# Sums of x2 in five tasks between the first groups' steps, later statistics, and another block order in the second feed-forward product

## The chip, the cores and the metric

The kernel runs on one core of one Trainium2 chip. The metric is device microseconds of one launch, from the kernel's first to its last instruction and what lies around them. The core has a matrix engine (TensorE, in the profile PE, with its weight loads as PEld), two engines for elementwise work (VectorE, DVE, and ScalarE, ACT), GpSimd (POOL), and SyncE, whose queue (SPq) issues every DMA of this kernel. Each engine executes its instructions in the order in which the program was laid out.

## The reference, cut to what matters

One transformer layer on x of 1024 tokens by 1024 features, float32: a mixer (an mLSTM and a latent attention), a cross-attention into 256 memory tokens, and a feed-forward part. The change touches the end of the cross-attention and the feed-forward part:

```
x = x + memory_cross_attention(rmsnorm(x, norm_x_g[l]), mem_n, ...)    # its last product is o @ wo_x
h = rmsnorm(x, norm_ffn_g[l])
x = x + jnp.square(jax.nn.relu(h @ w_ff1[l])) @ w_ff2[l]               # 1024 -> 4096 -> 1024
```

## The kernel before

Activations lie feature by token, split in two token halves of 512 (`h` = 0, 1) and eight feature blocks of 128 (`k`). x2, the input of the feed-forward part, is in the tiles `res` (`R[h][k]`). Every float32 product is made of three passes on rounded halves ("hi" and "lo"): `split` writes hi on ACT (a CAST) and lo on DVE (a subtraction), and three matmuls use hi·hi, hi·lo and lo·hi.

**Both feed-forward products are block products in seven multiplications instead of eight.** x2 is cut in four blocks B11, B21 (token half 0) and B12, B22 (token half 1); the scheme needs the sums T1 = B12 − B11, T2 = B22 − T1, T3 = B22 − B12, T4 = B21 − T2 of them, and sums S1 to S4 of the blocks of the weight.

- `wo_groups` (L1194): the last product of the cross-attention. Its eviction writes `res`, stores it to `x2d` in DRAM and adds up squares in `st`: ACT writes a square into the single buffer `sq`, DVE adds it to `st`. After the last block it gives two tasks to the weaver: `xs` (`stats_x2`, L1217: four small matmuls `vps`, a VectorE step into `v`, a power on GpSimd into `r`) and `xn` (`norm_x2`, L1221).
- `norm_x2`: four VectorE steps and a matmul (`xdg`, `bps`) spread 1/rms over the tokens, `res` is scaled, and the halves of the blocks are made: for h = 0 those of B11 and B21 (`xB`), for h = 1 T1, T2, T3, B22, T4 (`xT`, and `xB` for B22) in one task of 20 steps.
- The weaver (L59) is a planner with its own costs. It runs when the program is written out and decides in which order the steps of tasks are laid among the steps of the main product. `until` runs tasks until a named one is done. A scheduler behind it then fixes the order on each engine, and moves an instruction forward where it takes the engine to be idle.
- `lead` (L1472): the first three of eight groups of 512 hidden features (`q`) begin with the multiplications of B11 and B21, which need h = 0 alone: 12 steps of 12 matmuls (`gf<-xB,w1u`).
- `ffn` (L1483): waits for the whole task `xn1`, then takes the other steps: T1, T2, T3, B22, T4 of groups 0 to 2, and all seven of groups 3 to 7. `prep` (L1535) makes the halves `w1u` of a step's weights two steps ahead. `combos` (L1507) loads blocks of w_ff1 (`w1r`) and makes the sums of a group: S1 = A21 + A22 (the tile `S`), S3 = A11 − A21, S2 = A11 − S1, S4 = A12 − S2, the last three in place. Blocks A11 and A12 of group 0 are loaded a second time, into buffers (tag "W") that hold `res`. Squared hidden values go to DRAM as seven planes `hd`.
- The second product has seven multiplications of 16 units (`units`, i and c), 12 matmuls each (`gf<-hu,w2u`). `prep2` (L1624) makes the halves `hu` and `w2u` of a unit two units ahead; `combos2` (L1633) makes the sums of w_ff2 in place (`w2r<-w2r`); `evac2` (L1673) adds the four banks of a multiplication into the results Y, U, Z, W (`acc`) after its last unit. `PL` is the order of the multiplications; the first two add up in the same banks, each other one starts new banks, taken in turn from two pools of four.

Of the kernel before, what the change touches and what calls it, by code (L numbers as in the profile page):

```python
# [18 lines left out]
P = 128  # L19
NK = 8  # L20
# [161 lines left out]
class Trunk:  # L182
# [160 lines left out]
    def run(self):  # L343
# [70 lines left out]
        with ExitStack() as lctx:  # L414
# [14 lines left out]
            self.lead_load(0)  # L429
            wv.done["ffa"] = wv.now  # L430
# [763 lines left out]
    def wo_groups(self, h):  # L1194

        V, R = self.V, self.R
        loc = {}

        def evac(g):
# [21 lines left out]
    def norm_x2(self, h):  # L1221
# [3 lines left out]
        t = self.big("raw", "xdg")  # L1225
        self.diag4(t[:, 0], self.r2[h])
        self.spread(t[:, 1], t[:, 0])
        rb = t[:, 1]
        yield 0.85, {}

        def norm(k):
            V.scalar_tensor_tensor(R[h][k], R[h][k], self.vec("gffn", k), rb, ALU.mult, ALU.mult)

        def halves(n, src):
            u = self.big("x1" if h else "x0", "x" + n, F32R)
            self.split(u[:, 0], u[:, 1], src)
            X.setdefault(n, []).append(u)

        def sub(o, a, b):
            V.tensor_tensor(o, a, b, ALU.subtract)  # L1240
            return o

        B11, B21, B12, B22 = R[0][:4], R[0][4:], R[1][:4], R[1][4:]
        if h == 0:
            for k in range(NK):
                norm(k)
                halves("B11" if k < 4 else "B21", R[0][k])
                yield 0.0, {}
            return
        for k in range(4):  # L1250
            norm(k)
            halves("T1", sub(B11[k], B12[k], B11[k]))
            yield 0.0, {}
        for k in range(4):
            norm(4 + k)
            halves("T2", sub(B11[k], B22[k], B11[k]))
            yield 0.0, {}
        for k in range(4):
            halves("T3", sub(B12[k], B22[k], B12[k]))
            yield 0.0, {}  # L1260
        for k in range(4):
            halves("B22", B22[k])
            yield 0.0, {}
        for k in range(4):
            halves("T4", sub(B21[k], B21[k], B11[k]))
            yield 0.0, {}
# [171 lines left out]
    def lead_load(self, q):  # L1438
        if q == 0:
            self.X, self.lw, self.lu, self.C = {}, {}, {}, {}  # L1440
        if q < self.LEAD:
            self.lw[q] = [self.w1_tile(q, 11, "raw"), self.w1_tile(q, 12, "raw")]

    def lead_prep(self, n):
        q, i = n // 4, n % 4
        if q < self.LEAD:
            if i == 2:
                self.lead_load(q + 1)
            self.lu[n] = self.w1_halves(self.lw[q][i // 2], i % 2)
# [22 lines left out]
    def lead(self):  # L1472
        self.lead_prep(0)
        self.lead_prep(1)
        for n in range(4 * self.LEAD):
            self.lead_prep(n + 2)
            q, i, e = n // 4, n % 4 // 2, n % 2
            if n == 0:
                yield ["xn0"]
            self.early(q, i, e, self.lu.pop(n))  # L1480
            yield 2.72

    def ffn(self):  # L1483
        V, A, T, S = self.V, self.A, self.T, self.S
        self.wv.weave(self.lead(), 1.0)
        self.wv.until(["xn1"])
        X, C, W = self.X, self.C, {}

        def load(q, b):
            tag = "raw" if q == 0 and b in (21, 22) else "W"  # L1490
            W[q, b] = self.w1_tile(q, b, tag)
# [8 lines left out]
        steps = [(q, i, e) for q in range(self.NQ) for i in range(2 if q < self.LEAD else 0, 7) for e in range(2)]  # L1500
        first = {q: min(n for n, s in enumerate(steps) if s[0] == q) for q in range(self.NQ)}
        us, late = {}, {}
# [3 lines left out]

        def combos(q):  # L1507

            n = first[q] + (0 if q >= self.LEAD else -4)

            def s1():
                t = self.big("raw" if q == 0 else "W", "S1", F32, (P, 4, 256))
                V.tensor_tensor(t, W[q, 21], W[q, 22], ALU.add)
# [7 lines left out]
            w = lambda b: W[q, b]  # L1521
            at(n - 6, lambda: load(q, 11))
            at(n - 5, lambda: load(q, 12))
            at(n - 3, lambda: load(q, 21))
            at(n - 1, lambda: load(q, 22))
# [9 lines left out]
        def prep(n):  # L1535
            if n < len(steps):
                q, i, e = steps[n]
                a = ORDER[i][0]
                us[n] = self.w1_halves(W[q, int(a[1:]) if a[0] == "A" else a], e)
# [61 lines left out]
        PL = (("11", 0), ("12", 1), ("22", 3), ("S1", 4), ("S3", 6), ("S2", 5), ("S4", 2))  # L1601
        B, hr, u2 = {}, {}, {}

        def load_b(n):

            b, j = ("11", "12", "22", "21")[n // 8], n % 8
# [26 lines left out]
        def combos2(i, c):  # L1633

            if c % 2 == 0 or i < 2:
                return
            j = c // 2 - 1 if i == 2 else c // 2
            for j in ([j] if j >= 0 else []) + ([7] if i == 2 and c == 15 else []):
                if i == 2:
                    V.tensor_tensor(B["22", j], B["21", j], B["22", j], ALU.add)  # L1640
                    B["S1", j] = B["22", j]
                elif i == 3:
                    B["S3", j] = sub(B["21", j], B["11", j], B["21", j])
                elif i == 4:
                    B["S2", j] = sub(B["11", j], B["S1", j], B["11", j])
                elif i == 5:
                    B["S4", j] = sub(B["12", j], B["12", j], B["S2", j])
# [19 lines left out]
        def mms(i, c, o, w, h):  # L1667
            for n, (x, y) in enumerate(PASSES):
                go_on = i == 1
                T.matmul(banks[o], lhsT=w[:, x, o * P:(o + 1) * P], rhs=h[:, y, :],  # L1670
                         start=not go_on and c == 0 and n == 0, stop=c == 15 and n == 2, skip_group_check=go_on)

        def evac2(i, o):  # L1673
            U, Y, Z, R = (acc[a][o] for a in "UYZW")
            ps = banks[o]
            if i == 0:
                A.copy(U, ps)
            elif i == 1:
                add(R, ps, R)
                store(o, "W", 0, 0)  # L1680
                S.dma_start(R, self.x2d[1, 4 + o])
            elif i == 2:
                add(Y, ps, Y)
            elif i == 3:
                add(Z, ps, Z)
                add(R, ps, R)
            elif i == 4:
                add(R, ps, R)
                add(Y, ps, Y)
            elif i == 5:  # L1690
                add(U, ps, U)
                add(R, U, R)
                store(o, "W", 1, 1)
                add(Y, U, Y)
                store(o, "Y", 1, 0)
                add(Z, U, Z)
            else:
                for q in (slice(0, 256), slice(256, 512)) if o == 3 else (slice(0, HT),):
                    add(Z[:, q], ps[:, q], Z[:, q])
                    store(o, "Z", 0, 1, q)  # L1700
# [7 lines left out]
        for f in late.pop(0, []):  # L1708
            f()
        prep(0)  # L1710
        prep(1)
        for n, (q, i, e) in enumerate(steps):
# [87 lines left out]
```

## Time and profile before

| | us |
|---|---|
| median of 3 runs (lowest, highest) | 1281.69 (1280.64, 1283.23) |
| profiled execution | 1284.04 |
| its span, first to last instruction | 1282.0 |
| TensorE busy | 1238.5 |
| VectorE busy | 901.4 |
| ScalarE busy | 664.8 |

The profile lists per engine the busy time, and per instruction its start, its length, and how long the engine stood idle before it and what ended that. Instructions alike that follow each other are merged in a row ("x8"). PEclk is the TensorE clock that was granted: 1.00 is 2.4 GHz, 0.50 is 1.2 GHz.

### The profile page before, as it was taken

Reading aid. Unit: us, or ns where it says so; the run is one execution under the profiler, and the core shown is the slowest. Engines: PE = TensorE matmul, PEld = TensorE weight load, DVE = VectorE, ACT = ScalarE, POOL = GpSimd, SP = SyncE. Lnnn points to the kernel's source line nnn. Section 1 sums busy time; section 2 is a strip of 40 time slices with the busy share of each in tenths; the row PEclk is TensorE's granted clock in tenths of the full one; section 3 lists DMA queues with packets and bytes.
Section 4 is the critical chain, followed back from the end, with each engine's and each line's share of the span. In section 5 each row is a group of like instructions: output and inputs, shape, how many; then the busy total and the mean of one; then the engine's idle time right before and its main releaser. Section 6 shows DMA issues by size and latency. Waiting matters only on the chain.

```text
span 1282.0 us, 17593 instructions
## 1 busy us (share of the span) xinstructions
PE 1238.5 (97%) x6030; PEld 1015.8 (79%) x6030; DVE 901.4 (70%) x1931; ACT 664.8 (52%) x1540; POOL 72.3 (6%) x90
## 2 busy tenths in 40 slices
PE   7999999999999999999897999999999999999998
PEld 6777777777888878888775888888888888888877
DVE  5876797898766556668689776576656459974674
ACT  6466645688555445546454444544444443444432
POOL 1100100243100010000000000000000000000000
PEclk9999999999999999999898999999999999999999
DMA  7245433312134364333245554444399934333341
GB/s 244 82 126 187 142 90 108 132 51 83 51 107 125 106 194 128 108 123 124 74 132 180 181 194 151 167 145 143 120 324 314 331 100 163 99 99 99 99 148 65
DMA packets 113168, 180.65 MB, mean 141 GB/s; under 512 B 8472, under 2 KB 40120, under 8 KB 113080
## 3 DMA queue, kind: packets, MB, share of 16 engines
q1 hardware_dynamic: 113080, 179.55, 42.6%
q8 instruction: 47, 0.77, 0.3%
q14 instruction: 41, 0.34, 0.1%
HBM read 134.41 MB, written 45.11 MB: 140 GB/s over the span
## 4 chain that ended last, share of the span: by engine, by line
PE 78%; DVE 8%; DMA 4%; issue 4%; ACT 3%; POOL 1%; SPq 0%; POOLq 0%; DVEq 0%; ACTq 0%
PE gf L56 45%; PE g L56 20%; PE pAS L56 3%; PE po L56 2%; DMA xr<-in_xT_dram 1%; DVE res L56 1%; PE pPT L56 1%; DMA xt<-in_x_dram 1%; DVE wu L56 1%; PE pxo L56 1%; DVE acc L56 1%; PE pq L56 1%; PE pxS L56 1%; PE qkps L56 1%; ACT wu L56 1%
## 5 line engine op out<-in xcount | busy, mean ns | idle before, releaser
L56 PE MATMUL gf<-hu,w2u 128*128 128x512 f32 x1344 | 305.4, 389 | 3.6 <-DVE hu L56 3.2
L56 PEld LDWEIGHTS gf<-hu,w2u 128*128 128x128 f32 x1344 | 252.1, 188 | 56.8 <-DVE hu L56 3.6
L56 PE MATMUL gf<-xT,w1u 128*128 128x512 f32 x768 | 182.9, 398 | 8.4 <-ACT w1u L56 8.4
L56 PEld LDWEIGHTS gf<-xT,w1u 128*128 128x128 f32 x768 | 145.4, 190 | 43.7 <-ACT w1u L56 8.8
L56 ACT CAST hu<-hr 128x512 fp32r<-128x512 f32 x112 | 69.8, 624 | 171.9 <-PE gf L56 171.9
L56 PE MATMUL g<-wu,xs 128*128 128x512 f32 (+1 forms) x576 | 145.0, 404 | 9.1 <-ACT wu L56 6.1
L56 DVE TENSOR_TENSOR hu<-hr,hu 128x512 fp32r<-128x512 f32 x112 | 77.3, 690 | 100.6 <-ACT hu L56 100.6
L56 PEld LDWEIGHTS g<-wu,xs 128*128 128x128 f32 x576 | 108.7, 193 | 36.2 <-ACT wu L56 6.7
L56 PE MATMUL gf<-xB,w1u 128*128 128x512 f32 x576 | 135.2, 392 | 0.0
L56 PEld LDWEIGHTS gf<-xB,w1u 128*128 128x128 f32 x576 | 108.0, 188 | 24.4 <-issue 0.5
L56 ACT CAST w1u<-w1r 128x512 fp32r<-128x512 f32 x96 | 59.1, 619 | 118.1 <-PE gf L56 115.7
L56 PE MATMUL g<-yT,wu 128*128 128x512 f32 x384 | 107.5, 411 | 1.4 <-ACT yT L56 1.4
L56 DVE TENSOR_TENSOR wu<-raw,wu 128x512 fp32r<-128x512 f32 (+1 forms) x112 | 75.9, 679 | 46.7 <-ACT wu L56 46.3
L56 ACT CAST wu<-raw 128x512 fp32r<-128x512 f32 (+1 forms) x112 | 68.3, 613 | 67.0 <-PE g L56 50.1
L56 DVE TENSOR_TENSOR w1u<-w1r,w1u 128x512 fp32r<-128x512 f32 x96 | 66.1, 689 | 35.4 <-ACT w1u L56 35.1
L56 DVE TENSOR_TENSOR c<-gf,c 128x512 f32<-128x512 f32 x80 | 55.1, 688 | 44.7 <-PE gf L56 44.6
L56 PEld LDWEIGHTS g<-yT,wu 128*128 128x128 f32 x384 | 68.7, 192 | 13.4 <-ACT yT L56 1.9
L56 DVE TENSOR_TENSOR w2u<-w2r,w2u 128x512 fp32r<-128x512 f32 x112 | 76.7, 685 | 0.0
L56 ACT CAST w2u<-w2r 128x512 fp32r<-128x512 f32 x112 | 68.9, 615 | 4.4 <-PE gf L56 4.4
L56 ACT ACTIVATE c<-c 128x1024 f32<-128x1024 f32 x56 | 59.5, 1062 | 8.6 <-DVE c L56 6.2
L56 PE MATMUL g<-xs,wu 128*128 128x512 f32 x192 | 48.4, 402 | 0.4 <-ACT mraw L56 0.4
L56 PE MATMUL g<-oT,wu 128*128 128x512 f32 x192 | 47.2, 398 | 0.4 <-ACT oT L56 0.4
(430 smaller groups left out, 1876.2 us busy)
## 6 DMA issues: line engine op xcount, KB each, us to landing
hd<-c SPq DMA_DIRECT2D x56, 512.0 KB, 3.5
hr<-hd SPq DMA_DIRECT2D x56, 512.0 KB, 3.6
w1r<-in_w_dram SPq DMA_DIRECT2D x38, 512.0 KB, 3.8
w2r<-in_w_dram SPq DMA_DIRECT2D x32, 512.0 KB, 7.1
raw<-in_w_in_dram SPq DMA_DIRECT2D x48, 256.0 KB, 2.9
raw<-in_w_out_dram SPq DMA_DIRECT2D x32, 256.0 KB, 3.0
xr<-in_xT_dram SPq DMA_DIRECT2D x16, 256.0 KB, 3.4
xt<-in_x_dram SPq DMA_DIRECT2D x16, 256.0 KB, 3.4
```

What stands on the lines that cost most here:

```text
L56: return f(*args, **kw)
```

## The change

The change has three parts.

1. **Statistics.** `xs0` may not begin before the planner's time of "ffa" plus 3.5 us; the other work that is laid there comes first.
2. **Sums of x2.** `norm_x2` becomes `sums_x2`, two tasks for h = 0 (B1, B2) and five for h = 1 (T1, T2, T3, B22, T4), in a chain. The step loops of `lead` and `ffn` become one loop `body` that is woven with these tasks: in groups 0 to 2 a step asks only for the task of its own block (`NEED`). The steps stay in the same order. The scratch `xdg` moves from the tag "raw" to "L2". The sums S3, S2, S4 of group 0, and the second loads of its A11 and A12, come one to several steps later in the program.
3. **Second product.** The multiplications run in another order of planes and weight blocks; the sums of w_ff2 follow it. Multiplications 2, 4 and 5 (numbers of the new order: i = 1, 3, 4) add up in one set of banks, 3 and 6 in the other. The evictions have 33 additions on VectorE in place of 45 and 4 copies on ScalarE; the partial result that was stored and read back is gone, and the residuals are read one result at a time.

```diff
-            self.lead_load(0)
-            wv.done["ffa"] = wv.now
+            self.ffn_setup()
+            wv.done["ffa"] = wv.now + 3.5
...
-                    self.wv.add(f"xs{h}", self.stats_x2(h, loc["st"]), prio=self.prio["xs"], res=dict(m=1))
-                    self.wv.add(f"xn{h}", self.norm_x2(h), [f"xs{h}", "xb2" if h else "ffa"], prio=self.prio["xn"],
-                                res=dict(m=1))
+                    self.wv.add(f"xs{h}", self.stats_x2(h, loc["st"]), prio=self.prio["xs"], res=dict(m=1),
+                                need=[] if h else ["ffa"])
+                    for n, kk in (("B1", 0), ("B2", 4)) if h == 0 else (("T1", 0), ("T2", 4), ("T3", 0), ("B22", 4), ("T4", 0)):
+                        self.wv.add("x" + n, self.sums_x2(h, n, kk), self.x2need + [f"xs{h}", "xb2" if h else "ffa"],
+                                    prio=self.prio["xn"], res={} if self.x2need else dict(m=1))
+                        self.x2need = ["x" + n]
...
-        self.wv.weave(self.lead(), 1.0)
-        self.wv.until(["xn1"])
...
-            at(n + 1, put("S3", lambda: sub(w(21), w(11), w(21))))
-            at(n + 2, put("S2", lambda: sub(w(11), w("S1"), w(11))))
-            at(n + 3, put("S4", lambda: sub(w(12), w(12), w("S2"))))
+            at(n + 1 if q else n + 2, put("S3", lambda: sub(w(21), w(11), w(21))))
+            at(n + 2 if q else n + 3, put("S2", lambda: sub(w(11), W[q, "S1"], w(11))))
+            at(n + 3 if q else n + 4, put("S4", lambda: sub(w(12), w(12), W[q, "S2"])))
...
-        PL = (("11", 0), ("12", 1), ("22", 3), ("S1", 4), ("S3", 6), ("S2", 5), ("S4", 2))
+        PL = (("22", 3), ("11", 0), ("S1", 4), ("S2", 5), ("S3", 6), ("S4", 2), ("12", 1))
+        CONT = (3, 4, 5)
+        SET = (1, 0, 1, 0, 0, 1, 0)
...
             elif i == 5:
-                add(U, ps, U)
-                add(R, U, R)
-                store(o, "W", 1, 1)
-                add(Y, U, Y)
-                store(o, "Y", 1, 0)
-                add(Z, U, Z)
+                add(Z, ps, Z)
+                store(o, "Z", 0, 1)
...
+        NEED = (["xB1"], ["xB2"], ["xT1"], ["xT2"], ["xT3"], ["xB22"], ["xT4"])
+
+        def body():
+            for n, (q, i, e) in enumerate(steps):
...
+                if q < self.LEAD:
+                    yield NEED[i]
+                make(n, q, i, e)
+                yield 2.72
+
+        self.wv.weave(body(), 1.0)
...
-            if c == 0 and i != 1:
-                banks[:] = [self.bank(i % 2 == 0) for _ in range(4)]
+            if c == 0 and i not in CONT:
+                banks[SET[i]] = [self.bank(SET[i]) for _ in range(4)]
```

Three places show what moves. **TensorE at the statistics of token half 0** (`vps`), between the transposes `pxT`, the products `pxo` of the last two cross-attention blocks, and the products `g` of the last half of `wo_x`; rows with − are before, with + now:

```order
 L56 MATMUL pxT<-ident,xP 128x128 x8
-L56 MATMUL vps<-ones,st_6882 128x1 x4
 L56 MATMUL pxo<-xPT,vmem 128x128 x8
 L56 MATMUL pxT<-ident,xP 128x128 x8
 L56 MATMUL pxo<-xPT,vmem 128x128 x8
+L56 MATMUL vps<-ones,st_6882 128x1 x2
 L56 MATMUL g<-oT_6725,wu 128x512 x12
+L56 MATMUL g<-oT_6726,wu 128x512 x6
+L56 MATMUL vps<-ones,st_6882 128x1 x2
```

The `vps` stood ahead of two rounds of `pxo` and one of `pxT`, and now stands behind them, half of it inside the products `g`.

**VectorE at the sums of token half 1.** Before, `S` (the sum S1 of the weights of group 0, used by the first step on T1) stands behind all of these sums (`res<-res`):

```order
L56 TENSOR_TENSOR res<-res 128x512 x2
L56 TENSOR_TENSOR xB_7696<-res,xB_7696 128x512
L56 TENSOR_TENSOR xT_7700<-res,xT_7700 128x512
L56 TENSOR_TENSOR xT_7704<-res,xT_7704 128x512
L56 TENSOR_TENSOR xT_7708<-res,xT_7708 128x512
L56 TENSOR_TENSOR res<-res 128x512
L56 TENSOR_TENSOR S_7723<-w1r 128x1024
L56 TENSOR_TENSOR xT_7712<-res,xT_7712 128x512
L56 TENSOR_TENSOR w1r<-w1r 128x1024
L56 TENSOR_TENSOR w1u<-S_7723,w1u 128x512
L56 TENSOR_TENSOR w1r<-S_7723,w1r 128x1024
```

Now `S` stands among the halves of T2 (`xT_7718` and `xT_7723` are two of the four); the other sums of the weights (`w1r<-w1r` is S3, `w1r<-S` is S2, the next `w1r<-w1r` is S4) follow behind T3 and among B22:

```order
L56 TENSOR_TENSOR S_7614<-w1r 128x1024
L56 TENSOR_TENSOR xT_7718<-res,xT_7718 128x512
L56 TENSOR_TENSOR xT_7723<-res,xT_7723 128x512
L56 TENSOR_TENSOR w1u<-S_7614,w1u 128x512
```

```order
L56 TENSOR_TENSOR xT_7774<-res,xT_7774 128x512
L56 TENSOR_TENSOR xT_7778<-res,xT_7778 128x512
L56 TENSOR_TENSOR res<-res 128x512 x3
L56 TENSOR_TENSOR xT_7782<-res,xT_7782 128x512
L56 TENSOR_TENSOR xB_7799<-res,xB_7799 128x512
L56 TENSOR_TENSOR w1r<-w1r 128x1024
L56 TENSOR_TENSOR xB_7824<-res,xB_7824 128x512
L56 TENSOR_TENSOR w1r<-S_7614,w1r 128x1024
L56 TENSOR_TENSOR xB_7830<-res,xB_7830 128x512
L56 TENSOR_TENSOR w1r<-w1r 128x1024
L56 TENSOR_TENSOR w1u<-w1r,w1u 128x512 x4
```

Between these two fences stand 8 instructions. `S` moved ahead of the last sum of T2 and of all of T3, B22 and T4; S3, S2 and S4 stand among the halves of B22, ahead of the halves of T4 and of the last two sums T4.

**VectorE at the end of the sixth multiplication of the second product**, before:

```order
L56 TENSOR_TENSOR hu<-hr,hu 128x512
L56 TENSOR_TENSOR acc<-gf,acc 128x512 x2
L56 TENSOR_TENSOR acc<-acc 128x512 x6
L56 TENSOR_TENSOR acc<-gf,acc 128x512 x2
L56 TENSOR_TENSOR acc<-acc 128x512 x6
L56 TENSOR_TENSOR w2u<-w2r,w2u 128x512
```

and now, at the same place, with eight additions at the end of the fifth:

```order
L56 TENSOR_TENSOR hu<-hr,hu 128x512
L56 TENSOR_TENSOR acc<-gf,acc 128x512 x4
L56 TENSOR_TENSOR w2u<-w2r,w2u 128x512
L56 TENSOR_TENSOR hu<-hr,hu 128x512
L56 TENSOR_TENSOR w2u<-w2r,w2u 128x512
```

Sixteen additions between two halves became four. Elsewhere in the second product, 16 of the 32 sums of w_ff2 (`w2r<-w2r`) now stand between the halves of the first 22 units, from behind the tenth `w2u` on, where before only `hu` and `w2u` stand.

## Rows read from the trace of the kernel before

**Rows 1.** The page, busy time of the engines
```profile
PE 1238.5 (97%) x6030; PEld 1015.8 (79%) x6030; DVE 901.4 (70%) x1931; ACT 664.8 (52%) x1540; POOL 72.3 (6%) x90
```

**Rows 2.** Waits of TensorE after 600 us: total, times, longest
```profile
PE gf L56 <- ACT w1u L56: 8.4, 1, 8.4
PE vps L56 <- DVE st L56: 6.3, 1, 6.3
PE gf L56 <- DVE hu L56: 3.2, 1, 3.2
PE gf L56 <- DVE acc L56: 0.4, 1, 0.4
```

**Rows 3.** Windows: stretch, its length, busy time of engines, PEclk, DMA share, GB/s
```profile
617.00:619.00 2.00, 2.00 (x16) 1.89 (x14) 0.29 (x1) 0.54 (x2) 0.00 (x0) 0.80 0.00 0
...
622.00:645.00 23.00, 22.90 (x98) 18.24 (x98) 21.09 (x40) 13.49 (x26) 0.00 (x0) 1.00 0.17 58
...
692.20:693.20 1.00, 1.00 (x4) 0.76 (x4) 1.00 (x2) 0.96 (x2) 0.00 (x0) 0.65 0.43 146
...
1237.00:1241.00 4.00, 0.81 (x4) 0.34 (x4) 4.00 (x7) 0.71 (x2) 0.00 (x0) 1.00 0.70 262
```

**Rows 4.** Timeline at the first wait: start, length, engine, instruction, idle before
```profile
605.75 1.03 PE L56 MATMUL pxT<-ident,xP 128*128 128x128 f32 x8
...
607.17 1.08 ACT L56 COPY xPT<-pxT 128x512 f32<-128x512 f32 x2
...
612.31 0.69 DVE L56 TENSOR_TENSOR st<-st,sq 128x512 f32<-128x512 f32 x1 [0.69 <-ACT sq L56]
613.05 1.87 PE L56 MATMUL vps<-ones,st 128*128 128x1 f32 x8 [6.27 <-DVE st L56]
...
619.37 2.38 PE L56 MATMUL pxo<-xPT,vmem 128*128 128x128 f32 x16 [0.24 <-ACT xPT L56]
...
622.10 3.02 PE L56 MATMUL g<-oT,wu 128*128 128x512 f32 x12 [0.35 <-ACT oT L56]
```

**Rows 5.** Timeline around the second wait; last two: loads of w1r, KB and landing
```profile
652.85 1.02 PE L56 MATMUL vps<-ones,st 128*128 128x1 f32 x8
...
656.68 24.18 PE L56 MATMUL gf<-xB,w1u 128*128 128x512 f32 x104
...
672.18 0.69 DVE L56 TENSOR_TENSOR res<-res 128x512 f32<-128x512 f32 x1
...
687.29 1.22 DVE L56 TENSOR_TENSOR S<-w1r 128x1024 f32<-128x1024 f32 x1
...
688.54 1.14 ACT L56 CAST w1u<-S 128x512 fp32r<-128x512 f32 x2 [0.52 <-DVE S L56]
...
689.21 18.68 PE L56 MATMUL gf<-xT,w1u 128*128 128x512 f32 x72 [8.36 <-ACT w1u L56]
...
w1r<-in_w_dram SPq DMA_DIRECT2D x38, 512.0 KB, 3.8
...
DMA to landing us min/median/max: 6.7/7.5/7.7
```

**Rows 6.** Timeline of the second product; fourth row: landing of w2r, 955 to 1060 us
```profile
980.30 0.41 SPq L1610 DMA_DIRECT2D w2r<-in_w_dram  x1
...
986.31 0.69 DVE L56 TENSOR_TENSOR hu<-hr,hu 128x512 fp32r<-128x512 f32 x1 [1.42 <-ACT hu L56]
...
1052.92 2.49 DVE L56 TENSOR_TENSOR w2r<-w2r 128x1024 f32<-128x1024 f32 x2
...
DMA to landing us min/median/max: 5.0/6.9/7.9
...
1142.64 4.87 DVE L56 TENSOR_TENSOR acc<-gf,acc 128x512 f32<-128x512 f32 x8
...
1235.68 3.69 DVE L56 TENSOR_TENSOR acc<-acc 128x512 f32<-128x512 f32 x6
...
1240.63 37.51 PE L56 MATMUL gf<-hu,w2u 128*128 128x512 f32 x164 [3.19 <-DVE hu L56]
```

More of the change, by code (lines that the diff above doesn't have):

```diff
@@ L1219, in stats_x2, with sums_x2, sub @@
         yield 0.3, {}
-    def norm_x2(self, h):
+    def sums_x2(self, h, n, k0):
         V, R, X = self.V, self.R, self.X
[L1225 to L1234, printed above, removed]
+        if n in ("B1", "T1"):
+            t = self.big("L2", "xdg")
+            self.diag4(t[:, 0], self.r2[h])
+            self.spread(t[:, 1], t[:, 0])
+            self.rb2 = t[:, 1]
+            yield 0.85, {}
+        rb = self.rb2
+        def sub(o, a, b):
+            V.tensor_tensor(o, a, b, ALU.subtract)
+        B11, B21, B12, B22 = R[0][:4], R[0][4:], R[1][:4], R[1][4:]
+        for k in range(4):
+            if n in ("B1", "B2", "T1", "T2"):
+                r = R[h][k0 + k]
+                V.scalar_tensor_tensor(r, r, self.vec("gffn", k0 + k), rb, ALU.mult, ALU.mult)
+            if n == "T1":
+                sub(B11[k], B12[k], B11[k])
+            elif n == "T2":
+                sub(B11[k], B22[k], B11[k])
+            elif n == "T3":
+                sub(B12[k], B22[k], B12[k])
+            elif n == "T4":
+                sub(B21[k], B21[k], B11[k])
+            src = {"B1": B11, "B2": B21, "T1": B11, "T2": B11, "T3": B12, "B22": B22, "T4": B21}[n][k]
@@ L1235, in halves @@
             u = self.big("x1" if h else "x0", "x" + n, F32R)
             self.split(u[:, 0], u[:, 1], src)
[L1237 to L1265, printed above, removed]
+            X.setdefault({"B1": "B11", "B2": "B21"}.get(n, n), []).append(u)
@@ L1470, in plane @@
         self.S.dma_start(self.hd[i][2 * q:2 * q + 2].rearrange("n p c -> p n c"), t)
[L1472 to L1481, printed above, removed]
     def ffn(self):
         V, A, T, S = self.V, self.A, self.T, self.S
-        self.wv.weave(self.lead(), 1.0)
-        self.wv.until(["xn1"])
[L1487 to L1491, printed above, removed]
+        X, C, W, steps, us = self.X, self.C, self.W, self.steps, self.us
         def sub(o, a, b):
@@ L1633, in combos2 @@
         def combos2(i, c):
[L1635 removed]
+            if c % 2 == 0:
                 return
[L1637 to L1639 removed]
+            j = c // 2 - 1
+            for j in ([j] if j >= 0 else []) + ([7] if c == 15 else []):
+                if i == 1:
                     V.tensor_tensor(B["22", j], B["21", j], B["22", j], ALU.add)
                     B["S1", j] = B["22", j]
+                elif i == 2:
+                    B["S2", j] = sub(B["22", j], B["S1", j], B["11", j])
                 elif i == 3:
@@ L1707, in ffn @@
         at(N - 2, lambda: load_h(3))
[L1708 to L1712, printed above, removed]
-            for f in late.pop(n, []) if n else []:
-                f()
-            prep(n + 2)
-            if n >= N - 2:
-                prep2(n - N + 2)
-            make(n, q, i, e)
+        NEED = (["xB1"], ["xB2"], ["xT1"], ["xT2"], ["xT3"], ["xB22"], ["xT4"])
+        def body():
+            for n, (q, i, e) in enumerate(steps):
+                if n == 0:
+                    prep(0)
+                    prep(1)
+                for f in late.pop(n, []):
+                    f()
+                prep(n + 2)
+                if n >= N - 2:
+                    prep2(n - N + 2)
+                if q < self.LEAD:
[3 more added lines that the diff above has]
+        self.wv.weave(body(), 1.0)
         nb = 8
-        banks = [None] * 4
+        banks = [None, None]
         for n, (i, c) in enumerate(units):
```

88 lines of the change are left out of this document (46 added, 42 removed).

## The prediction, made before the changed kernel ran

> **What bounds the kernel now.** TensorE, by its own busy time: 1238.5 us of the span [rows 1]. So an edit gains only where TensorE stands still or runs at half clock. I read TensorE's waits first, for the part of the span that the change touches, from 600 us on: four, of 8.4, 6.3, 3.2 and 0.4 us, 18.3 in all [rows 2]. Then the windows around them, for the clock. After the 6.27 us wait the granted clock is 0.80 in 617 to 619, after the 8.36 us wait it is 0.65 in 692.2 to 693.2, and after the 3.19 us wait it is 1.00 [rows 3]. With two levels, 1.00 (2.4 GHz) and 0.50 (1.2 GHz), half clock ended 0.8 us into the first window and 0.7 into the second: it ran from 613.05 to 617.8 and from 689.2 to 692.9, 4.8 and 3.7 us, of which half is lost, 2.4 and 1.8. What can be won at most is 18.3 + 4.2 = 22.5 us. Last I read who is late in each wait, in the timelines [rows 4 to 6]; the number of matmuls stays as it is.
>
> **Statistics (term A).** The `vps` wait for `st`, whose last addition starts at 612.31: each of its four squares waits for the buffer of the one before, and VectorE idles 0.69 us each time [rows 4]. Meanwhile `pxo`, `pxT`, `pxo` and the products `g` stand behind `vps` on TensorE's queue, although the copies `xPT` end at 608.25. The change puts `vps` behind them. Walked by hand: `pxo` from 608.3; a round of 16 took 2.38 us at full clock with a wait of 0.24 in it [rows 4], so 2.2, to about 610.5; `pxT` 1.03, to 611.6; its copy and the next round, 612.3 to 614.6. The squares now alternate with the small `oT` steps on both engines, so `st` is done about 614.9; two `vps` and the first `oT` let `g` start at about 615.6 instead of 622.10: 6.5 us earlier. Of this, 1.2 us go back: half of `vps` (1.02 us whole at full clock [rows 5]) and a wait for `xdg` now lie inside `g`, and VectorE, which was busy 21.1 of 23.0 us in 622 to 645 [rows 3], has the same work for a shorter stretch. Its rows up to the second `vps`, 35 steps from 624.7 on at 0.62 (an estimate a little above the 0.60 that eight in a row take each [rows 6]) and 1.2 of waiting for evictions, give 647.6 for that `vps`, against 652.85 [rows 5]. So A = 5.3. Bounds: 2.9, if the clock falls all the same, and 6.5, if nothing is given back.
>
> **Sums (term B).** Everything from the second `vps` to the step on T1 keeps its distance, so I stay in the times of before. TensorE ends the steps on B11 and B21 at 680.85 [rows 5]. `S` stood behind all sums of x2 and ran at 687.29; now it stands right behind the sum that ran at 672.18, so it runs at 672.8, its halves are there by 677.7, and the 24 matmuls on T1 (0.233 each, from 24.18 us for 104 [rows 5], so 5.6 us) run from 680.85 to 686.4 without a wait. Then comes a new wait, the one thing the part does not remove: T2 needs S2 = A11 − S1, A11 needs a buffer that T3's first two halves set free, at 681.4 by the count of the rows, then a load, then the sums S3 and S2 (1.22 us each, a half between them) and the cast on ACT. The load: 3.8 us is the median of all 38, but 6.7 to 7.7 for the five that were issued together from 681.4 on [rows 5]. I take 4.5, nearer the first, because this load now goes out ahead of the others. A11 is there at 686.0, S2 at 689.0, the first half for T2 at 689.6. VectorE makes S4 before the lo halves of T2, so TensorE runs seven matmuls on hi halves and is in full flow from 691.3, which counts as a start at 689.7. T3 ends 48 matmuls later, at 700.9. Before, it ended at 707.9 (689.21 + 18.68 [rows 5]). So B = 7.0 by this walk; A12's load, which S4 needs and which is issued at 684.5 together with others, may be late by up to 2, so I take B = 6.5. Bounds: 3.0, with both loads at 7.5 us and some half clock, and 7.5. Behind T3, the steps on B22 and T4 find their halves ready by the same count (the last half of T4 at about 709, used at about 709), and the evictions into `c22`, which wait for buffers of `res` that T4 sets free, are 3 us ahead of their use.
>
> **Second product (term C).** The wait of 3.19 us comes from 16 additions in a row on VectorE (3.69 us for the last six [rows 6]) while `w2u` and `hu` of the next units stand behind. With 8 additions, 4.87 us, the row of before at 1142.64 has no wait on TensorE behind it [rows 2, 6]; the changed kernel has 8 at most. The 0.4 us came from a second set of banks out of the pool that had just been used, with two sums of weights in front of the evictions; the new sets alternate. So 3.6 us go. Against that, 16 sums of w_ff2 now lie in the first 22 units. Up to there VectorE has 16 × 1.2 + 25 × 0.60 + 4 × 0.60 = 36.6 us of work from about 987.5 on (pitches from [rows 6]); the half `hu` that unit 21 needs must be there by 1026.5, 39.0 later, and 2.4 us of cover are left for waiting on loads of `w2r`. The first such load is issued at about 980.3, as a load in that place is now, and lands 5.0 to 7.9 us later [rows 6]: 985 to 988, and the next, at about 984.8, by 993, used at about 991. I expect 1 to 3 us of waiting on VectorE and 0.6 on TensorE. C = 3.0; bounds 0 and 3.6. The four copies on ACT and the store and reload that go lie beside other work and are worth nothing.
>
> **The sum.** A + B + C = 5.3 + 6.5 + 3.0 = 14.8. Against the profiled execution, 1284.04 us: 1269.2. Its span is 1282.0, and 2.0 lie around it. The median of the runs is 1281.69, 2.35 below that execution, so I predict 1266.9 for the median.
>
> **Rivals.** *S2 is the new late one.* Both loads take 7.5 us and the clock falls in the gap, which is then over 5 us instead of 3: B = 3.0, the median 1270.4. For: the landings of 6.7 to 7.7 [rows 5]. Against: fewer loads are in flight.
>
> *The clock falls at the first place all the same.* TensorE there has transposes, small products and three gaps of 0.7 to 1.5 us in 9 us. A = 5.3 − 2.4 = 2.9 and the median 1269.3. Against it: 3.19 us of standing still left the clock at 1.00 [rows 3], but there full products ran on both sides. The Trainium skill ("TensorE: Matmul & The Clock Gate", Part 4) says that transposes do not count as activity for the clock; by that rule this case is the likelier, and the sum would be 12.4 instead of 14.8. No row before shows a stretch of this make-up, so its chance stays low.
>
> *The sums of w_ff2 hold up the second product.* VectorE takes its queue in order, so a sum whose load is late holds back `hu` and `w2u` of all later units. Once the 2.4 us of cover are used, each further microsecond reaches TensorE. With 4 us beyond it C = −0.4, and the median is 1270.3. **The slower outcome** is this one: it decides from 15.4 us of waiting beyond the cover (14.8 + 0.6), that is 2.2 us for each of the eight sums that need the third block, (15.4 + 2.4) / 8. Loads landing in 10 us instead of 7 would do it; at 3 us each, 24 − 2.4 − 15.4 = 6 us slower, 1288. Against: the slowest of 23 took 7.9 [rows 6].
>
> *It doesn't do what it says.* If the second loads of A11 and A12 hold SP's queue or the sums wait for each other, both waits are only moved: A and B vanish but for 1 us, C is 3.0 less 2, and the median is about 1280. Against: the order of instructions shows `S` and `vps` moved.
>
> **How the numbers follow.** The forecast, 1266.9, gets 0.62, with its own range of 1263.8 to 1269.5; S2 late 0.14, half clock at the first place 0.09, sums in the second product without a loss overall 0.06, no effect 0.05, slower 0.04. The range of 1263.5 to 1273.0 takes in the first four, and two of the middle cases together (1273). Below 1263.5 is only what needs all three upper bounds, 17.6. About 0.2%, 2.6 us, is what a measurement of this kernel can tell from no change. So: faster 0.91, same 0.05, slower 0.04.
>
> **What would show it.** Right: the wait of `vps` for `st` gone, PEclk 1.00 from 606 on; the first `gf<-xT` right behind the last `gf<-xB`, and one wait of about 3 us some 24 matmuls later, ended by `w1u`; no wait for `hu` at the end of the second product. Wrong, A: PEclk 0.50 around 612 to 618, or the second `vps` waiting for `st` over 1 us. Wrong, B: that wait over 5 us, or others at T4. Wrong, C: waits of `w2u` or `hu` between units 9 and 22, with VectorE waiting for `w2r` loads. The prediction as a whole fails if the middle of the first product, which had no wait from 741 to 969, gets any: then the moved loads cost what I took as free.

## The result, and the profile after

The changed kernel takes 1265.89 us (median of 4 runs, 1264.90 to 1267.75) against 1282.46 us for the kernel before (4 runs, 1280.64 to 1284.07). The ratio is 0.9863, 95% interval 0.9846 to 0.9879: 16.6 us faster. The forecast was 1266.9 us, range 1263.5 to 1273.0. Its profiled execution took 1264.90 us, with a span of 1263.1.

The page of the changed kernel, busy time; it answers to [rows 1]:

```profile
PE 1234.6 (98%) x6030; PEld 1011.2 (80%) x6030; DVE 894.9 (71%) x1919; ACT 662.0 (52%) x1536; POOL 72.6 (6%) x90
```

The number of matmuls is the same, and TensorE's busy time fell by 3.9 us only. Most of the rest of the gain is time in which it stood still. Its waits from 600 us on (total, times, longest), where [rows 2] had 8.4, 6.3, 3.2 and 0.4:

```profile
PE gf L56 <- ACT w1u L56: 2.1, 1, 2.1
PE pxo L56 <- ACT xPT L56: 1.3, 2, 1.0
PE bps L56 <- DVE xdg L56: 1.0, 2, 0.5
PE vps L56 <- DVE st L56: 0.4, 1, 0.4
```

The four old waits are gone; what is left is one of 2.1 us for `w1u` and small ones of 2.7 us in all. (The trace of before has three small ones too, which [rows 2] leaves out: `bps` 0.5, `g` 0.4, `pxo` 0.2.) TensorE's timeline of the changed kernel at the three places (start, length, instruction, idle time before it in brackets), which answers to [rows 4 to 6]:

```profile
603.70 1.03 PE L56 MATMUL pxT<-ident,xP 128*128 128x128 f32 x8
605.75 2.32 PE L56 MATMUL pxo<-xPT,vmem 128*128 128x128 f32 x16 [1.02 <-ACT xPT L56]
...
611.91 0.58 PE L56 MATMUL vps<-ones,st 128*128 128x1 f32 x4 [0.36 <-DVE st L56]
612.35 4.35 PE L56 MATMUL g<-oT,wu 128*128 128x512 f32 x18
...
644.39 1.05 PE L56 MATMUL vps<-ones,st 128*128 128x1 f32 x8
...
672.25 5.76 PE L56 MATMUL gf<-xT,w1u 128*128 128x512 f32 x24
680.10 13.17 PE L56 MATMUL gf<-xT,w1u 128*128 128x512 f32 x48 [2.09 <-ACT w1u L56]
...
954.46 304.82 PE L56 MATMUL gf<-hu,w2u 128*128 128x512 f32 x1344
```

`vps` now waits 0.36 us instead of 6.27. The products on T1 follow B11's and B21's at once, and T2 waits 2.09. The second product is one row of 1344 matmuls without a gap. The windows (PEclk is the number before the last two) tell where the clock stood:

```profile
609.00:613.00 4.00, 3.40 (x23) 2.96 (x24) 3.17 (x8) 2.50 (x9) 0.00 (x0) 1.00 0.97 329
613.00:619.00 6.00, 6.00 (x30) 5.00 (x29) 2.65 (x7) 3.49 (x8) 1.38 (x1) 1.00 0.22 77
...
680.00:683.00 3.00, 2.90 (x7) 1.80 (x7) 1.74 (x2) 1.61 (x4) 0.00 (x0) 0.58 0.88 305
680.50:683.90 3.40, 3.39 (x9) 2.17 (x8) 2.64 (x4) 1.11 (x3) 0.00 (x0) 0.50 0.64 220
683.00:685.00 2.00, 1.99 (x8) 1.56 (x8) 2.00 (x5) 0.00 (x0) 0.00 (x0) 0.77 0.11 28
685.00:690.00 5.00, 5.00 (x23) 4.08 (x22) 4.62 (x8) 1.25 (x2) 0.00 (x0) 1.00 0.64 202
```

At the first place it stays at 1.00, where [rows 3] had 0.80. Behind the wait at T2, which ends at 680.10, it falls to its lower level from 680.5 to 683.9. Only seven matmuls begin between 680 and 683, and that is the pace of this level: five of them in a row begin 0.43 us apart, where 0.23 us is the pace at 1.00. What T2 waited for is seen on SyncE's queue and VectorE (same columns as the timeline above; the first line is the issue of A11's load, the second begins with the issue of A12's):

```profile
672.88 0.37 SPq L1412 DMA_DIRECT2D w1r<-in_w_dram  x1
...
675.29 10.60 SPq L1412 DMA_DIRECT2D w1r<-in_w_dram  x5
...
664.36 1.21 DVE L56 TENSOR_TENSOR S<-w1r 128x1024 f32<-128x1024 f32 x1
...
676.43 1.23 DVE L56 TENSOR_TENSOR w1r<-w1r 128x1024 f32<-128x1024 f32 x1
...
678.18 1.22 DVE L56 TENSOR_TENSOR w1r<-S,w1r 128x1024 f32<-128x1024 f32 x1
...
681.26 1.23 DVE L56 TENSOR_TENSOR w1r<-w1r 128x1024 f32<-128x1024 f32 x1 [1.26 <-DMA w1r<-in_w_dram]
682.40 2.49 DVE L56 TENSOR_TENSOR w1u<-w1r,w1u 128x512 fp32r<-128x512 f32 x4
...
988.06 1.23 DVE L56 TENSOR_TENSOR w2r<-w2r 128x1024 f32<-128x1024 f32 x1 [1.03 <-DMA w2r<-in_w_dram]
```

The lines from 664.36 to 681.26 are S1, S3, S2 and S4 of group 0. S3 and S2 found A11 there, and the first half that T2 needs is made from S2, which ends at 679.40. S4 waited 1.26 us for A12's load, and the low halves that T2 needs stand behind it. On TensorE this late S4 shows in one place: the eighth matmul on T2 begins 0.63 us behind the seventh instead of 0.43, 0.2 us lost. The rest of its lateness lies under the half clock: at full clock the first seven would have been through about 1.4 us sooner (an estimate from the two paces), and TensorE would have stood still for the low halves. The last line is a sum of w_ff2 in the second product, which also waits for a load, with no wait on TensorE behind it.

Span against span the two executions differ by 18.9 us, and 2.05 of that are not the change's: the `pxT` ahead of the first wait begins at 605.75 before [rows 4] and at 603.70 after, with the same instructions in the same order up to there (TensorE, VectorE, ScalarE and GpSimd). So the experiments are compared by stretches between landmarks of TensorE's timeline: that `pxT` (the expectations call it the second transposes); the first matmul on B11; the first on T1; the first on B22; the first of the second product; its last.

### The profile page after: what moved, and what is told of

Its sections match the earlier page's. It is cut to its first block, busy times and chain, and to the rows that moved or that the text cites. A ratio compares the mean times of both kernels' runs of the same rounds, so it can differ in the third digit from the quotient of the medians.

```text
span 1263.1 us, 17573 instructions
## 1 busy us (share of the span) xinstructions
PE 1234.6 (98%) x6030; PEld 1011.2 (80%) x6030; DVE 894.9 (71%) x1919; ACT 662.0 (52%) x1536; POOL 72.6 (6%) x90
## 4 chain that ended last, share of the span: by engine, by line
PE 81%; DVE 7%; DMA 4%; issue 4%; ACT 3%; POOL 1%; SPq 0%; POOLq 0%; DVEq 0%; ACTq 0%
PE gf L56 46%; PE g L56 21%; PE pAS L56 3%; PE po L56 2%; DMA xr<-in_xT_dram 1%; PE pPT L56 1%; DVE res L56 1%; PE pxo L56 1%; DMA xt<-in_x_dram 1%; DVE wu L56 1%; PE pq L56 1%; ACT wu L56 1%; PE pyT L56 1%; PE pxS L56 1%; PE qkps L56 1%
```

## The experiments

Starts, differences of starts, and the end of the last matmul, in us, worked out from TensorE's timeline of each trace; the ratio is that of the times, against runs of before on the same chip:

| kernel | that pxT at | to B11 (A) | B11 to T1 | T1 to B22 | B11 to B22 (B) | B22 to second product | second product (C) | ratio to before, 95% |
|---|---|---|---|---|---|---|---|---|
| before | 605.75 | 39.33 | 44.13 | 18.52 | 62.65 | 261.39 | 309.02 | |
| before, again | 604.92 | 39.90 | 44.14 | 18.79 | 62.93 | 261.39 | 309.06 | 0.9993 (0.9977–1.0009) |
| C alone | 606.09 | 40.43 | 44.14 | 19.44 | 63.58 | 261.39 | 304.82 | 0.9953 (0.9936–0.9970) |
| A alone | 605.52 | 33.00 | 44.10 | 19.63 | 63.73 | 261.37 | 310.46 | 0.9954 (0.9938–0.9970) |
| A and C | 604.00 | 33.03 | 44.07 | 18.43 | 62.50 | 261.39 | 304.82 | 0.9896 (0.9877–0.9915) |
| B and C | 603.91 | 39.48 | 35.60 | 19.04 | 54.64 | 261.63 | 304.82 | 0.9879 (0.9862–0.9896) |
| changed (A, B, C) | 603.70 | 33.02 | 35.53 | 20.86 | 56.39 | 261.35 | 304.82 | 0.9863 (0.9846–0.9879) |
| changed, again | 607.00 | 33.03 | 35.56 | 20.85 | 56.41 | 261.36 | 304.82 | 0.9850 (0.9831–0.9869) |
| changed, third | 603.82 | 33.05 | 35.53 | 20.77 | 56.30 | 261.37 | 304.82 | 0.9851 (0.9828–0.9875) |
| early loads | 604.38 | 33.01 | 35.55 | 18.14 | 53.69 | 261.47 | 304.82 | 0.9827 (0.9809–0.9846) |
| early loads, again | 606.25 | 33.05 | 35.55 | 18.14 | 53.69 | 261.43 | 304.82 | 0.9834 (0.9812–0.9856) |
| and S1 on GpSimd | 604.36 | 33.05 | 35.54 | 23.69 | 59.23 | 264.27 | 304.82 | 0.9889 (0.9871–0.9906) |
| and other buffers for c12, c22 | 604.89 | 33.01 | 35.57 | 16.79 | 52.36 | 266.53 | 304.82 | 0.9858 (0.9841–0.9874) |

**C alone.** The hunks of the second product, on the kernel before:

```diff
-        PL = (("11", 0), ("12", 1), ("22", 3), ("S1", 4), ("S3", 6), ("S2", 5), ("S4", 2))
+        PL = (("22", 3), ("11", 0), ("S1", 4), ("S2", 5), ("S3", 6), ("S4", 2), ("12", 1))
+        CONT = (3, 4, 5)
+        SET = (1, 0, 1, 0, 0, 1, 0)
...
```

> The kernel before with the change in the second product alone (order 4 1 5 6 7 3 2, two sets of banks, the later loads and sums of w_ff2). Theory: three separate terms that add up, A (statistics) 6.4 us, B (sums in tasks) 6.2, C (second product) 4.2, as the two traces give them. Then this kernel keeps the waits of 6.3 us (vps for st) and 8.4 us (w1u) and loses the 3.2 and 0.4 us ones; the stretch of the second product is 304.8 us instead of 309.0; the time is 4.2 us below before (1282.5 to 1278.3, ratio 0.997). Rival: part of the 4.2 comes from what A and B left in front of the second product (buffers and loads that are earlier); then the stretch is 305.4 us or more, or waits for hu or w2u show in it.

The second product takes 304.82 us, to the hundredth what it takes in the changed kernel; the other two waits stand as before. TensorE's waits from 600 us on in this kernel:

```profile
PE gf L56 <- ACT w1u L56: 8.4, 1, 8.4
PE vps L56 <- DVE st L56: 6.3, 1, 6.3
```

C is worth 4.2 us against the first trace of before, and needs nothing of A or B.

**A alone.**

```diff
-            wv.done["ffa"] = wv.now
+            wv.done["ffa"] = wv.now + 3.5
...
-                    self.wv.add(f"xs{h}", self.stats_x2(h, loc["st"]), prio=self.prio["xs"], res=dict(m=1))
+                    self.wv.add(f"xs{h}", self.stats_x2(h, loc["st"]), prio=self.prio["xs"], res=dict(m=1),
+                                need=[] if h else ["ffa"])
```

> The kernel before with the statistics' two edits alone (the normalisation's due time 3.5 us later, and the squares of the first half held back to it). Theory of separate terms: the wait of vps for st goes, the clock stays at 1.00 from 606 to 619, the second vps comes 6 us earlier, the wait at T1 stays at about 8.4 us with its stretch of half clock: 6.4 us below before (1276.1, ratio 0.995). Rival, VectorE carries the stretch: the sums of x2 end no earlier than before because VectorE, not TensorE, sets them; then the wait at T1 grows by what was won at vps, and the gain is 0 to 2 us.

The stretch to B11 falls to 33.00 us, 6.3 below the first trace of before, and B11 to T1 stays at 44.10: the wait of 8.4 us moves along whole and does not grow, so VectorE does not carry that stretch. The trace brought one thing that was not asked for. Its wait for `hu` in the second product is the old one of 3.19 us, but here the clock fell behind it (window of this kernel):

```profile
1235.00:1238.00 3.00, 2.87 (x7) 2.29 (x8) 3.00 (x6) 0.00 (x0) 0.00 (x0) 0.50 0.12 36
```

and the second product took 310.46 us instead of 309.02.

**A and C, B left out.** The edits of the two kernels above together.

> The kernel before with the statistics and the second product changed, and the sums of x2 as they were (A and C without B). Separate terms: only the wait of 8.4 us for w1u at T1, with its stretch of half clock, is left of the four; the time is 10.6 us below before (6.4 + 4.2; ratio 0.992) and 6.2 above the changed kernel (1.005). Rival, B is worth more than its 6.2 because the clock fell at T2 in the changed kernel's trace and need not: up to 9 us above the changed kernel.

Of the four old waits the 8.4 us one alone is left. B11 to B22 takes 62.50 us, so that B, beside A and C, is worth 6.2 (62.50 − 56.3). In time this kernel is 0.9896, the changed one 0.9850 in the same comparison: 0.5%, 5.9 us, as the separate terms have it (6.2). Against before the times give 13.4 us where the terms have 10.6, and the stretches 10.6 (6.30 + 0.15 + 4.20).

**B and C, A taken out of the changed kernel.** The two edits of A put back.

> The changed kernel with the statistics put back where they were (sums in tasks and second product as changed, B and C). Separate terms: the wait of vps for st is back with about 6.3 us and the granted clock near 0.8 in the two microseconds behind it, and the time is 6.4 us above the changed kernel (1272.3, ratio 0.992 to before). Rival, the terms depend on each other: with x2 later by 6 us against the loads, A11's and A12's second loads have more time, the wait at T2 is smaller, and the time is only 3 to 5 us above the changed kernel.

The wait for `st` is back, and the stretch to B11 takes 39.48 us again. But B11 to B22 takes 54.64, 1.7 us less than beside A. TensorE's timeline of this kernel, and then the window behind T2's wait:

```profile
678.99 5.76 PE L56 MATMUL gf<-xT,w1u 128*128 128x512 f32 x24
686.57 11.63 PE L56 MATMUL gf<-xT,w1u 128*128 128x512 f32 x48 [1.82 <-ACT w1u L56]
```

```profile
687.00:692.00 5.00, 5.00 (x23) 3.76 (x22) 5.00 (x9) 1.70 (x4) 0.00 (x0) 1.00 0.97 315
```

T2 waits almost as long (1.82 against 2.09), yet 48 matmuls take 11.63 us instead of 13.17, and the clock stays at 1.00. S4 here waits for no load. This is the one trace of this kernel. So the rival holds in part: A is worth 6.3 without B, and 6.46 − 1.75 + 0.28 = 5.0 with it, the middle figure being B11 to B22 and the last the stretch behind it. B is worth 8.0 without A (62.65 − 54.64) and 6.2 with it; the kernels without B spread from 62.50 to 63.73 in this stretch, by the length of their half clock. In time this kernel lies 0.0016 to 0.0029 above the three ratios of the changed kernel, 2.1 to 3.7 us, with intervals that overlap; the figure of 5.0 rests on the stretches alone.

**Early loads of A11 and A12.** On the changed kernel; S3, S2 and S4 of group 0 at the steps of the other groups.

```diff
             if q == 0:
-                at(n, lambda: self.load_w1(q, 11))
-                at(n + 1, lambda: self.load_w1(q, 12))
+                at(2, lambda: self.load_w1(q, 11, "x1"))
+                at(3, lambda: self.load_w1(q, 12, "x1"))
...
-            at(n + 1 if q else n + 2, put("S3", lambda: sub(w(21), w(11), w(21))))
+            at(n + 1, put("S3", lambda: sub(w(21), w(11), w(21))))
...
```

> The changed kernel with one more edit: group 0's second loads of A11 and A12 go into two buffers of x2's sums (T4's last tiles take others later) and are issued some 6 steps earlier, and its sums S3, S2, S4 go one step earlier, as in the other groups. Theory: what is left at T2 (a wait of 2.09 us for w1u, seven matmuls on high halves with a wait for low ones, the clock at 0.58 and 0.77 up to 685) comes from the late buffer and load of A11 and A12. Then T2 follows T1 with no wait over 0.3 us, the clock stays at 1.00, and the matmuls on B22 begin up to 3.9 us earlier: 1262.0 us, ratio 0.984 to before. Rival, VectorE is the bound there (it was busy without a gap from 675 to 680): the sums of weights that now run earlier push back the sums of x2 behind them, the wait moves to T2's or T3's own halves, and the gain is 0 to 1 us.

TensorE's timeline of this kernel, and then a window:

```profile
672.94 16.96 PE L56 MATMUL gf<-xT,w1u 128*128 128x512 f32 x72
691.08 5.82 PE L56 MATMUL gf<-xB,w1u 128*128 128x512 f32 x24 [1.18 <-DVE c L56]
```

```profile
672.00:691.00 19.00, 17.90 (x77) 14.08 (x75) 18.93 (x33) 12.51 (x22) 0.00 (x0) 1.00 0.42 138
```

T1, T2 and T3 run as one row of 72 matmuls, and the clock stays at 1.00. So the late loads, together with the later steps of the sums that they forced, were what T2 waited for; the two moved together here, and the run does not tell one from the other. (In the changed kernel A11's load landed 3.5 us after its issue, at 676.4, and S3 began at 676.43 on a VectorE that had been busy up to there.) VectorE is busy 18.93 of 19 us, and 1.18 us of the wait come back at B22: of 3.9 us, 2.7 are won. Both theories had a part in it.

**The same kernels traced again.** Before and changed in one comparison, changed and early loads in another.

> The kernel before, unchanged, traced a second time. It tells what of the difference between the first two traces belongs to one execution and not to the change: the second transposes begin at 605.75 us before and at 603.70 after, although the order of instructions up to there is the same, and the half-clock stretches behind a wait lasted 4.8 and 3.7 us in the first trace and another time in others. Theory, chance: the time up to those transposes spreads by 2 us and more from execution to execution, and this trace may show 604 as well as 606. Rival, it belongs to the kernel (its buffers lie elsewhere): 605.5 to 606.1 here again, as in the three traces with the feed-forward part of before. The ratio is 1.000 in both cases.

> The changed kernel, unchanged, traced a second time. Chance: the second transposes begin anywhere from 603.5 to 606. Rival, it belongs to the kernel: 603.7 to 604.4 again. The wait at T2 should be 2.1 us again; the clock after it was 0.58 and 0.77 for 5 us, while behind the 1.82 us wait at T2 of the kernel without A it stayed at 1.00: if that is chance, it may stay at 1.00 here, and the matmuls on T2 and T3 then take 11.6 us instead of 13.2. Ratio to before 0.986 from the first runs.

> The changed kernel a third time, beside the kernel with the early loads in the same comparison. The stretch from the first matmul on B11 to B22 should again be 56.4 us (a wait of 2.1 to 2.3 us at T2 with the clock down behind it); if the clock stays up this once, 54.9.

> The kernel with the early loads of A11 and A12 (two buffers as in the changed kernel) a second time, to size it against the changed kernel in the same comparison. Theory: the stretch from B11 to B22 is 53.7 us again, 2.7 us below the changed kernel, all others equal, so the ratio to before is 0.002 lower than that of the changed kernel. Rival: the first trace of it was a lucky one; then the stretch is 55 us or more.

The `pxT` ahead of the first wait begins, in the changed kernel, at 603.70, 607.00 and 603.82 us: chance, 3.3 us wide, and the 2.05 us of the first pair lie inside it. The clock has a part in it. Before and changed, between 139 and 143 and between 138 and 142 us, then the second trace of the changed kernel at two places:

```profile
139.00:143.00 4.00, 4.00 (x15) 3.46 (x15) 3.33 (x13) 0.98 (x3) 0.00 (x0) 0.62 0.10 27
...
138.00:142.00 4.00, 3.81 (x20) 3.10 (x21) 3.92 (x14) 2.11 (x9) 0.00 (x0) 1.00 0.22 67
...
127.00:130.00 3.00, 3.00 (x14) 2.18 (x15) 2.23 (x5) 1.99 (x4) 0.00 (x0) 0.53 0.79 265
267.00:270.00 3.00, 3.00 (x10) 2.31 (x9) 2.41 (x12) 1.72 (x5) 2.21 (x2) 0.52 0.01 4
```

Every trace has half clock near 480 us. The five with 3.4 us of it there and none elsewhere between 20 us and that `pxT` reach it at 603.70 to 604.38; the four with one more such stretch, before among them, reach it at 605.52 to 606.25, and the trace at 607.00 has two more. The other three have 6.8 us near 480 and reach it at 604.36 to 604.92. So the spread ahead of the change goes with how long the clock was low.

The wait at T2 and the fallen clock came in all three traces of the changed kernel: B11 to B22 took 56.39, 56.41 and 56.30. The gain of the early loads came twice too, 53.69 both times. In the last comparison the changed kernel has 0.9851 and the early loads 0.9834; the intervals overlap, so that the times alone do not separate them, but the stretches do, by 2.7 us each time.

**S1 on GpSimd, on top of the early loads.**

```diff
-                V.tensor_tensor(t, W[q, 21, False], W[q, 22, False], ALU.add)
+                (self.G if q == 0 else V).tensor_tensor(t, W[q, 21, False], W[q, 22, False], ALU.add)
```

> The kernel with the early loads of A11 and A12, with group 0's sum S1 on GpSimd instead of VectorE (one addition of 1.21 us on VectorE, 128 x 1024). Theory: with the loads early VectorE's queue is the bound from T1 to B22 (busy without a gap from 660 to 685), and the wait of 1.18 us that B22 has there for an addition into c is the rest of it. Then taking 1.21 us off that queue takes the wait away: B22 begins 52.5 us after the first matmul on B11 instead of 53.7, and the span is 1.2 us shorter. Rival: GpSimd takes so long for S1, or slows VectorE's additions beside it, that the wait only moves to T1 or stays: no gain, or up to 3 us lost.

GpSimd's, VectorE's and TensorE's timelines of this kernel, and a window:

```profile
664.61 3.38 POOL L56 TENSOR_TENSOR S<-w1r 128x1024 f32<-128x1024 f32 x1 [17.19 <-DVE w1u L56]
...
668.02 1.23 DVE L56 TENSOR_TENSOR w1r<-w1r 128x1024 f32<-128x1024 f32 x1 [2.29 <-POOL S L56]
...
695.81 2.48 DVE L56 TENSOR_TENSOR c<-gf,c 128x512 f32<-128x512 f32 x4
...
696.64 8.62 PE L56 MATMUL gf<-xB,w1u 128*128 128x512 f32 x24 [6.74 <-DVE c L56]
...
698.00:702.00 4.00, 4.00 (x11) 3.06 (x10) 2.63 (x4) 2.12 (x2) 0.00 (x0) 0.50 0.13 52
```

It lost 5.5 us from B11 to B22 and 2.8 behind it. S3 writes over A21, which S1 still reads, so VectorE stands for 2.29 us, more than the 1.22 it was spared. Then group 1's sums of weights slip in ahead of the four additions into `c`, which start at 695.81 instead of 690.25, and B22 waits 6.74 us and goes on at half clock (24 matmuls in 8.62 us, 5.76 at full clock). The Trainium skill (GPSIMD Engine Reference, section 3.1) gives a float32 addition of two tiles, 2048 elements wide, as 1.96 times slower there than on VectorE; here, 1024 wide, it is 3.38 against 1.22 us, 2.8 times, with VectorE idle for 2.29 of the 3.38 us.

**Other buffers for c12 and c22, on top of the early loads.**

```diff
-                t = self.big("M" if (h, k) in ((0, 4), (0, 6)) else "W", "res")
+                t = self.big("M" if (h, k) in ((1, 0), (1, 2)) else "W", "res")
```

> The kernel with the early loads of A11 and A12, S1 on VectorE again, with one more edit: the two buffers that c12 and c22 of group 0 take over are those of x2's tiles 0 to 3 of the second half (free after T3's halves) instead of tiles 4 to 7 of the first half (free only after T4's). Theory: the wait of 1.18 us that B22 has there is a wait for a buffer: c22's additions cannot be made before T4's sums have read the last of the old tiles, and VectorE is busy up to there. Then the additions come 3 to 6 us earlier on VectorE, B22 begins 52.5 us after the first matmul on B11 instead of 53.7, and the stretch from B22 to the second product stays at 261.4 to 261.6: the span is 1.2 us shorter at equal begin. Rival: the other tiles that now come free later are what the next loads of weights wait for (some leave later on SyncE's queue), and a wait of 1 to 3 us for w1u appears at T1 of group 1: no gain or a loss.

SyncE's queue in the kernel with the early loads alone, and then SyncE's queue, TensorE's and VectorE's timelines of this one, with a window:

```profile
678.76 11.97 SPq L1412 DMA_DIRECT2D w1r<-in_w_dram  x5
```

```profile
687.52 6.54 SPq L1412 DMA_DIRECT2D w1r<-in_w_dram  x4
...
690.26 5.76 PE L56 MATMUL gf<-xB,w1u 128*128 128x512 f32 x24
695.86 6.93 PE L56 MATMUL gf<-xT,w1u 128*128 128x512 f32 x28
705.55 17.77 PE L56 MATMUL gf<-xT,w1u 128*128 128x512 f32 x68 [2.75 <-ACT w1u L56]
...
699.55 1.23 DVE L56 TENSOR_TENSOR S<-w1r 128x1024 f32<-128x1024 f32 x1 [2.80 <-DMA w1r<-in_w_dram]
...
706.90:710.20 3.30, 3.30 (x9) 2.55 (x8) 3.30 (x5) 0.00 (x0) 0.00 (x0) 0.50 0.60 202
```

Both came true. B22's wait was one for a buffer: it is gone, and B11 to B22 takes 52.36 us. But the buffers given up for it are those that the next loads of weights use: the loads of `w1r` that left SyncE's queue from 678.76 us on leave from 687.52 on. Group 1's S1 waits 2.80 us for a load, TensorE 2.75 us for S1's halves, the clock falls to half behind that wait (last line), and the stretch behind B22 takes 266.5 instead of 261.4. The early loads with the old buffers stay the best kernel of these.

## Why the prediction was right, point by point

**The method held.** The four waits and their half clock were what could be won, and each of the three parts moved its own stretch. A + B + C came to 6.3 + 6.3 + 4.2 = 16.8 us by the first two traces, where 14.8 were predicted. The profiled time, 1264.90, lies 4.3 below the predicted 1269.2: 2.0 from the terms and about 2 from the chance ahead of that `pxT`. The medians moved by 16.6 us (1282.46 to 1265.89), 1.8 more than the sum, but the forecast started from 1281.69, 0.8 too low. That its error, 1.0 us, is smaller than the sum's is luck.

**A, 6.3 instead of 5.3.** The step that failed is the walk to `g`: 615.6 predicted, 614.40 measured (612.35 + 2.05, in the times of before). `st` was done sooner than walked, with 0.36 us of wait left. What was to be given back, 1.2 us, was 1.4 (7.7 won at `g`, 6.3 at B11), so that the second `vps` came at 646.44 against 647.6. The rival "the clock falls at the first place all the same" did not happen: 1.00 in 609 to 619, through gaps of 1.02, 0.24 and 0.36 us and two rounds of transposes. By the rule of the Trainium skill ("TensorE: Matmul & The Clock Gate", Part 4) it was the likelier; the stretch to B11 was 33.00 to 33.05 us in nine traces with A, at a granted clock of 1.00 in each, so no trace here bears it out for transposes with products between them.

**B, 6.2 instead of 6.5.** Counted from the second `vps`, the walk was close. `S` came at 19.97 us (walked 19.95) and T1 at 27.86 (28.0). A11's load left at 28.49 (28.55) and was there by 32.04, when S3 ran without a wait for it: 3.55 us at most, where 4.5 were taken. T2 so began 1.0 sooner than walked (35.71 against 36.75). Then the term that was only allowed for, A12's load late by up to 2, came on VectorE with 1.26 us, and cost TensorE 0.2 beside the half clock; in the second trace S4 waited 0.31 us only, and the stretch was the same (56.41). What was not in the sum is the clock: from T2's start to B22 are 13.0 us, where the walk had 11.3 to the end of T3. So B22 began at 48.72, where the walk's end of T3 had 48.05. That B came out within 0.3 us is luck: 1.0 us won at T2's start and 1.7 lost behind it come to 0.7 lost, close to the 0.5 that was set aside for A12. The rival "S2 is the new late one" had both loads take 7.5 us and the clock fall in a gap of over 5 us; A11's load was early, the wait was 2.1 to 2.3 us, and the clock fell all the same.

**C, 4.2 instead of 3.0.** Two steps failed, by 0.6 us each. The first is the 0.6 us lost to the sums of w_ff2. VectorE did wait for a load of `w2r`, 1.03 us at 988.06, the lower end of the 1 to 3 expected, and the 2.4 us of cover hid it. The second is the price of the two waits, which was taken as their idle time, 3.6 us, and was 4.2. TensorE's rows of before, three rows for the 1344 matmuls that are now one:

```profile
969.12 87.22 PE L56 MATMUL gf<-hu,w2u 128*128 128x512 f32 x384
1056.76 180.68 PE L56 MATMUL gf<-hu,w2u 128*128 128x512 f32 x796 [0.42 <-DVE acc L56]
1240.63 37.51 PE L56 MATMUL gf<-hu,w2u 128*128 128x512 f32 x164 [3.19 <-DVE hu L56]
```

The rows add up to 305.41 us of work, 0.59 more than the 304.82 of the one row. In a row a matmul begins 0.23 us after the one before, but each lasts 0.39, so the last one ahead of a wait runs on for 0.16 us before idle time is counted; and the first few behind each wait begin up to 0.11 us later than at that pace. Matmul by matmul against the changed kernel, the whole 4.2 us arises at these two places, 0.67 at the first and 3.52 at the second. The rival and its slower form did not come near.

**The whole.** The test set for it held: TensorE has no wait from B22 to the second product, 261.35 us against 261.39. The rival "it doesn't do what it says" fell with the first trace.

**What was missing is a link between the terms.** They were summed as if they were separate. A and C are; A and B are not quite: with A the clock fell behind T2's wait in all three traces, without A it did not in its one trace, and 1.7 us of A's worth go there. On VectorE what differs is A12's load. With A it leaves SyncE's queue at 675.29, 2.4 us behind A11's, when one of the sums of x2 has been made, and S4's turn comes 4.7 us later. Without A it follows A11's by 1.2 us, in one row:

```profile
679.01 1.57 SPq L1412 DMA_DIRECT2D w1r<-in_w_dram  x2
```

and S4's turn comes 6.2 us later. On TensorE this lateness lay under the half clock but for 0.2 us. What decided over the clock, the shorter wait (1.82 against 2.09 to 2.33 us) or chance, one trace cannot tell.

## What to carry to other kernels

Add up a change by stretches between landmarks that the change cannot move, not by spans: the same kernel traced again began its stretch 3.3 us later. When a wait is taken away, look at which buffer the next load or eviction needs: three times here (A11's, c22's, group 1's loads) the next wait was one for a buffer, and giving it another only pays if that buffer has no next user. An addition moved off a full engine must also free the tiles it reads in time, or the full engine waits for it.

## What the runs showed of the hardware that was not expected

The same wait did not always bring the clock down. Behind 3.19 or 3.20 us of standing still it stayed at 1.00 in two traces of the kernel before (second products of 309.02 and 309.06 us) and was 0.50 in that of A alone (310.46). Behind T2's wait of 2.1 to 2.3 us it fell in all three traces of the changed kernel, and behind the 2.75 us wait of the kernel with other buffers. Behind 1.82 us without A and behind 1.18 us with the early loads it stayed up. In the changed kernel it fell at most 0.4 us after T2's first matmul, and the seven matmuls in 3 us that follow are its effect: in the second trace they come at the same pace, though the first low half was there at 685.71 and the eighth matmul began at 686.84 only. Its window:

```profile
683.60:686.90 3.30, 3.22 (x8) 2.55 (x9) 3.02 (x5) 1.59 (x4) 0.00 (x0) 0.50 0.54 185
```

So the length of a wait alone does not decide, and these runs do not show what does. The stretch to B11 that holds the 6.3 us wait took 39.33 to 40.43 us in the four traces without A, by the length of the half-clock part. So half clock behind a wait is a term with a spread of 1 to 1.5 us, and not a constant.

A wait also cost more than the idle time that the profile lists for it: 0.25 us more at the one of 0.42 us and 0.33 at the one of 3.19, at a clock that stayed at 1.00.
